# A hybrid attention block on one core: queries and merged outputs come back from device memory in 32x32 squares, turned on VectorE instead of TensorE

## The chip, the core and the metric

The kernel runs on one core of a Trainium2 chip. The metric is device time in microseconds of that core, as the median of several executions. The core has a matrix engine (TensorE, PE in the profile; its weight loads are PEld), three engines for elementwise work (VectorE is DVE, ScalarE is ACT, GpSimd is POOL), and a queue engine that only issues transfers (SyncE, SP). ACT and POOL issue transfers too, each in the order of its own instructions.

## What is computed

One block of a sequence model, in float32, for 256 tokens of width 2048 and 256 context tokens. The input is normalised and modulated by a vector c, and one large projection `w_in` gives everything else: attention queries, keys, values and gates, the inputs of a gated recurrence (HGRN, 16 heads, forward and backward), and two merge gates.

```python
aq, ak, av, ag, hq, hff, hfb, hi, hg, ma, mb = split_columns(xn @ w_in[l])
...
q = apply_axial_rope(aq.reshape(B, n, ATT_HEADS, ATT_HEAD_DIM), cos, sin) * q_scale
...
att_branch = window_attention(q, k, v, k_c, v_c, sink_logits[l]) * jax.nn.silu(ag)
...
y_a = hg_branch @ w_o_hgrn_l
y_b = att_branch @ w_o_attn_l
y = jax.nn.sigmoid(m_a + b_m[0]) * y_a + jax.nn.sigmoid(m_b + b_m[1]) * y_b
return y @ w_out_l
...
h = h + gate * merge_and_project(...)
return rmsnorm(h, final_norm_gain)
```

Two results of this text matter here. The rotated queries `q` (256 tokens, 16 heads of 128) are needed with the head's 128 columns on the partitions, but come out of the projection with tokens on the partitions. The merged `y` (256 x 2048) likewise comes out by tokens, and `y @ w_out` needs it by columns. Both have to be transposed.

## The kernel before

**Weights.** Every weight is streamed once, in chunks of 128 x 1024 floats. SP loads a chunk into one of five `raw` buffers (L66). ACT rounds it to the matrix engine's 32-bit format (`wh`, L85, three buffers), and DVE subtracts to get the remainder (`wl`, L86, three buffers). Activations are split the same way into `xH` and `xL`. PE multiplies three of the four combinations: high by high and low activation by high weight alternate (L100, L101), and the products with the low weight come last in a chunk (L103), so that `wl` may come later than `wh`. In the column-wise projections the like lines are L154 and L157. A token-wise projection of 512 columns (`proj_tok_g`) is eight such chunks; each step of the generator is one chunk.

**Stages.** First the modulation, the norms and the first projections; then eight steps, one for each pair of HGRN heads (some 740 to 1250 us in the profile); then the attention of 16 heads, woven with the projection `w_o_hgrn` (to about 1405 us); then `part_b`, four column blocks of the projection `w_o_attn` with the merge into `y` (to about 1490 us); then `w_out` and the output.

**Side work in the head pairs.** The recurrence of a pair leaves PE free in between, and a list of seventeen blocks (`side_work`) fills it: the four query blocks (`attn_queries(j)`, 512 columns, that is four heads), the attention gates, merge gates and output gates. After the projection of a query block DVE rotates each of the two token tiles (`rope`, L1092, L1097 and L1100) into a tile `qr` of 128 tokens x 512. `send` (L527) then issues the write of `qr` to a buffer `qr_dr` in device memory on ACT's queue, at the first chunk of the following block. When this has been issued the fetch becomes a task. Tasks are run three times a pair (`tasks_on`): the first call of a task fetches the tile (L1151, on POOL's queue), the next one turns it. `turn_tile` makes four PE transposes of 128 x 128 into PSUM (L1116, tile `tkt`); ACT scales and rounds it (L1118), DVE takes the remainder (L1119), and POOL writes both to `q_dr` (L1157), from which the attention loads them.

**The merge.** In `part_b(n)` DVE multiplies the projection of each token tile by its gate (L1424) and adds it to `y[n]` (L1425), 128 tokens x 512 columns. PE turns both tiles, four transposes each (L1431, tile `tky`), and ACT and DVE split them from PSUM (L1105, L1106) into the places of `xH` and `xL` that `w_out` reads. The buffers of merged `y` are later filled with four pieces `lw` of `w_out` (L1473, on POOL's queue), which DVE multiplies by the output gate (L1477).

**What sets the order.** PE's instructions stand in the order in which the program writes them through the head pairs and the attention (`manual_schedule`). The order of ACT, DVE, POOL and SP is set by a scheduler ahead of time, from its own estimate of the run and from priorities; `issue_after` and `behind_chunk` hold an instruction behind the splits of the newest weight chunk. On the chip each engine works through its list in order, and an instruction that waits holds up all that stand behind it on its engine.

Of the kernel before, what the change touches and what calls it, by code (L numbers as in the profile page):

```python
# [38 lines left out]
def block_kernel(ctx: ExitStack, tc: tile.TileContext, x, c, cx, c_ctx, w_ada, b_ada, norm_gain, w_in,  # L39
# [126 lines left out]
        return o[:, :T]  # L166


    cs = few.tile([P, K_END], F32, name="cs")
    ident = cs[:, K_ID: K_ID + P]  # L170
    mk = pad.tile([P, len(LEVELS), 32], U8, name="mk")
# [59 lines left out]
    ma_dr = [dram.tile([P, 1024], F32, name=f"ma{n}") for n in range(4)]  # L231
    mb_dr = [dram.tile([P, 1024], F32, name=f"mb{n}") for n in range(4)]
    kv_dr = [[dram.tile([P, 1024], F32, name=f"kv{i}_{t}") for t in range(2)] for i in range(2)]
    qr_dr = [dram.tile([P, 1024], F32, name=f"qr{j}") for j in range(4)]
    q_dr = [[dram.tile([P, 1024], F32, name=f"q{j}_{z}") for z in range(2)] for j in range(4)]
    ag_dr = [dram.tile([P, 1024], F32, name=f"ag{j}") for j in range(4)]

    FIRST = (("F0", 2), ("F1", 1), ("F0", 2))
# [874 lines left out]
    def turn_tile(src, dst, scale=1.0):  # L1113
        tk = ps.tile([P, 512], F32, tag="tp", name="tkt")
        for j in range(4):
            pe.transpose(tk[:, j * P: (j + 1) * P], src[:, j * HD: (j + 1) * HD], ident)  # L1116
        tk = tk.rearrange("p (r c) -> p r c", r=dst[0].shape[1])
        act.activation(dst[0], tk, AF.Copy, scale=scale)  # L1118
        dve.scalar_tensor_tensor(dst[1], tk, scale, dst[0].bitcast(F32), op0=ALU.mult, op1=ALU.subtract)  # L1119
# [27 lines left out]
    def attn_queries(j):  # L1147

        def fetch(t):
            qr = base.tile([P, 512], F32, tag="sm", name="qr", bufs=3)  # L1150
            nc.gpsimd.dma_start(qr, qr_dr[j][:, t * 512: (t + 1) * 512])  # L1151

            def then():
                q = [XL[:, 8 + 4 * z + 2 * t: 10 + 4 * z + 2 * t, :] for z in range(2)]
                turn_tile(qr, q, HD ** -0.5)
                for z in range(2):
                    nc.gpsimd.dma_start(q_dr[j][z][:, t * 512: (t + 1) * 512].rearrange("p (r c) -> p r c", r=2),  # L1157
                                        q[z].bitcast(F32))
            return then

        bq = yield from proj_tok_g(w_in, C_Q + 512 * j, x_st, range(2))
        for t in range(2):
            qr = base.tile([P, 512], F32, tag="sm", name="qr", bufs=3)
            rope(qr.rearrange("p (r h d) -> p r h d", r=2, h=2), bq[t], t)
            outs.append((qr_dr[j][:, t * 512: (t + 1) * 512], qr, lambda t=t: fetch(t)))

    def attn_gates(j):
        for hf in range(2):
# [248 lines left out]
            nc.sync.dma_start(fg[0], row_bcast(fin_gain[:1024], 1024))  # L1417
        nc.gpsimd.dma_start(gt[t], row_bcast(gate_rows[8 * t: 8 * t + 8, :], 1024))

    def part_b(n):  # L1420
        by = proj_tok(w_oa, n * 512, x_st, range(2))
        for t in range(2):
            yt = base.tile([P, 512], F32, tag="sm", name="yt", bufs=3)
            dve.tensor_tensor(yt, by[t], sgb[n][:, t, :], op=ALU.mult)  # L1424
            dve.tensor_tensor(y[n][:, t, :], y[n][:, t, :], yt, op=ALU.add)  # L1425

        tks = [ps.tile([P, 4, P], F32, tag=tg, name="tky") for tg in ("tp", "o")]
        with tc.manual_schedule(engines={mybir.EngineType.PE}):
            for t in range(2):
                for i in range(4):  # L1430
                    pe.transpose(tks[t][:, i, :], y[n][:, t, i * P: (i + 1) * P], ident)  # L1431
        for t in range(2):
            ks = slice(4 * n, 4 * n + 4)
            split(XH[:, ks, t * P: (t + 1) * P], XL[:, ks, t * P: (t + 1) * P], tks[t])

    def load_merge(n):
        sgb[n] = gt_tile(n, [P, 2, 512], "sgb")
        nc.gpsimd.dma_start(sgb[n].rearrange("p t c -> p (t c)"), mb_dr[n])

    load_merge(0)  # L1440
    for n in range(4):
        if n < 3:
            load_merge(n + 1)
        part_b(n)


    def y_st(kt, t):
# [131 lines left out]
```

## Time and profile before

| what | value |
|---|---|
| median of three runs | 1571.25 us (1571.19 to 1571.34) |
| profiled execution, its own time | 1573.59 us |
| its span, first to last instruction | 1571.8 us |
| granted TensorE clock, mean | 0.998 |
| transferred over the span | 339.99 MB in 232812 packets, mean 216 GB/s |
| query transposes on PE (L1116, cs and qr) | 32, the first at 859.8, the last at 1185.4 us |
| y transposes on PE (L1431) | 32, the first at 1409.7, the last at 1483.3 us |
| fetch of a query tile, issue to landing, median | 5.3 us (256 KB) |

A row of the profile names line, engine and operation, then the tile written and the tiles read, and how often. "x4" behind a row of the chain means that four instructions in a row are taken together. Behind `<-` in square brackets stands what ended the idle time before an instruction. A DMA's row on an engine is the time for issuing it; the transfer itself goes on behind.

### The profile page before, as it was taken

Reading aid. Unit: us, or ns where it says so; the run is one execution under the profiler, and the core shown is the slowest. Engines: PE = TensorE matmul, PEld = TensorE weight load, DVE = VectorE, ACT = ScalarE, POOL = GpSimd, SP = SyncE. Lnnn points to the kernel's source line nnn. Section 1 sums busy time; section 2 is a strip of 40 time slices with the busy share of each in tenths; the row PEclk is TensorE's granted clock in tenths of the full one; section 3 lists DMA queues with packets and bytes.
Section 4 is the critical chain, followed back from the end, with each engine's and each line's share of the span. In section 5 each row is a group of like instructions: output and inputs, shape, how many; then the busy total and the mean of one; then the engine's idle time right before and its main releaser. Section 6 shows DMA issues by size and latency. Waiting matters only on the chain.

```text
span 1571.8 us, 25977 instructions
## 1 busy us (share of the span) xinstructions
PE 1548.8 (99%) x9946; PEld 1291.8 (82%) x9946; DVE 1199.1 (76%) x1758; ACT 880.2 (56%) x1380; POOL 157.0 (10%) x298
## 2 busy tenths in 40 slices
PE   7999999999999999999999999999999999999998
PEld 4558888888888888888888888788888888888887
DVE  4448987777787878878888897887987777757664
ACT  4326545444555555665666666566566767744442
POOL 2000001110100000011212221121121000000000
PEclk9999999999999999999999999999999999999999
DMA  9996645656644444477786896877787744458661
GB/s 370 386 387 238 215 160 156 181 160 186 148 121 134 135 134 134 141 266 245 239 267 218 292 290 231 272 242 250 232 270 245 272 154 156 161 183 286 221 206 69
DMA packets 232812, 339.99 MB, mean 216 GB/s; under 512 B 12368, under 2 KB 137712, under 8 KB 231920
## 3 DMA queue, kind: packets, MB, share of 16 engines
q1 hardware_dynamic: 201808, 249.54, 48.6%
q0 software_dynamic: 21376, 70.38, 14.4%
q10 hardware_dynamic: 9504, 18.42, 3.3%
q8 instruction: 78, 1.28, 0.3%
q14 instruction: 46, 0.38, 0.1%
HBM read 300.53 MB, written 37.76 MB: 215 GB/s over the span
## 4 chain that ended last, share of the span: by engine, by line
PE 88%; DMA 4%; DVE 4%; issue 2%; ACT 1%; SPq 0%; POOL 0%; POOLq 0%; DVEq 0%; ACTq 0%
PE pj L100 13%; PE pj L101 12%; PE pj L103 12%; PE pj L154 7%; PE pj L759 5%; PE pm L759 4%; PE pj L157 4%; DMA raw<-in_w_in_dram 3%; PE pm L665 3%; PE pj L665 3%; PE pj L763 3%; PE pm L763 2%; PE pj L427 2%; PE pa L323 2%; DVE wl L641 2%
## 5 line engine op out<-in xcount | busy, mean ns | idle before, releaser
L85 ACT ACTIVATE wh<-raw 128x1024 fp32r<-128x1024 f32 x284 | 299.3, 1059 | 253.9 <-PE pj L101 157.0
L86 DVE TENSOR_TENSOR wl<-raw,wh 128x1024 fp32r<-128x1024 f32 x284 | 344.6, 1220 | 114.2 <-ACT wh L85 112.6
L100 PE MATMUL pj<-wh,xHL 128*128 128x512 f32 (+1 forms) x768 | 298.6, 390 | 0.0
L101 PE MATMUL pj<-wh,xHL 128*128 128x512 f32 (+1 forms) x768 | 294.8, 385 | 0.0
L103 PE MATMUL pj<-wl,xHL 128*128 128x512 f32 (+1 forms) x768 | 202.7, 386 | 0.0
L100 PEld LDWEIGHTS pj<-wh,xHL 128*128 128x128 f32 x768 | 144.4, 188 | 28.2 <-ACT sg L219 0.6
L101 PEld LDWEIGHTS pj<-wh,xHL 128*128 128x128 f32 x768 | 144.4, 188 | 27.6
L103 PEld LDWEIGHTS pj<-wl,xHL 128*128 128x128 f32 x768 | 142.0, 188 | 29.0
L640 ACT ACTIVATE wh<-raw 128x1024 fp32r<-128x1024 f32 x100 | 105.8, 1058 | 93.7 <-PE pj L759 37.3
L640 ACT ACTIVATE wh<-T 128x1024 fp32r<-128x1024 f32 x75 | 79.6, 1062 | 109.9 <-DVE T L621 24.1
L641 DVE TENSOR_TENSOR wl<-raw,wh 128x1024 fp32r<-128x1024 f32 x100 | 121.5, 1219 | 21.2 <-ACT wh L640 20.9
L154 PE MATMUL pj<-xHL,wh 128*128 128x512 f32 x512 | 130.2, 396 | 0.0
L154 PEld LDWEIGHTS pj<-xHL,wh 128*128 128x128 f32 x512 | 92.4, 189 | 16.8
L641 DVE TENSOR_TENSOR wl<-T,wh 128x1024 fp32r<-128x1024 f32 x75 | 91.4, 1219 | 13.8 <-ACT wh L640 13.7
L157 PEld LDWEIGHTS pj<-xHL,wl 128*128 128x128 f32 x512 | 69.8, 190 | 5.2
L157 PE MATMUL pj<-xHL,wl 128*128 128x256 f32 x512 | 71.3, 282 | 0.0
L932 DVE TENSOR_TENSOR A<-A,X 128x512 f32<-128x512 f32 x96 | 61.6, 682 | 0.2
L759 PE MATMUL pj<-wh,S 128*128 128x512 f32 x224 | 55.3, 389 | 0.0
L665 PE MATMUL pm<-S,wh 128*128 128x512 f32 x208 | 52.6, 395 | 1.6 <-ACT s L672 1.6
L665 PE MATMUL pj<-S,wh 128*128 128x512 f32 x208 | 52.5, 394 | 0.4 <-ACT s L672 0.4
L100 PE MATMUL pj<-wh,bH 128*128 128x512 f32 x128 | 50.2, 392 | 0.0
L101 PE MATMUL pj<-wh,bL 128*128 128x512 f32 x128 | 50.1, 391 | 0.0
(348 smaller groups left out, 2823.4 us busy)
## 6 DMA issues: line engine op xcount, KB each, us to landing
raw<-in_w_in_dram SPq DMA_DIRECT2D x300, 512.0 KB, 4.7
raw<-in_w_ada_dram SPq DMA_DIRECT2D x64, 512.0 KB, 8.0
raw<-in_w_o_hgrn_dram SPq DMA_DIRECT2D x32, 512.0 KB, 3.7
raw<-in_w_o_attn_dram SPq DMA_DIRECT2D x32, 512.0 KB, 4.3
raw<-in_w_out_dram SPq DMA_DIRECT2D x28, 512.0 KB, 4.4
hgw<-in_w_ada_dram POOLq DMA_DIRECT2D x32, 256.0 KB, 4.6
so<-in_w_ada_dram POOLq DMA_DIRECT2D x32, 256.0 KB, 4.9
F<-F POOLq DMA_DIRECT2D x16, 512.0 KB, 6.5
```

The costliest lines, as they stand in the source:

```text
L85: last_hi[0] = act.activation(h[:, :n], raw[:, :n], AF.Copy).ins
L86: last_lo[0] = dve.tensor_tensor(lo[:, :n], raw[:, :n], h[:, :n].bitcast(F32), op=ALU.subtract).ins
L100: pe.matmul(o, s[0], m[0], start=first, stop=False)
L101: pe.matmul(o, s[1], m[0], start=False, stop=False)
L103: pe.matmul(o, s[0], m[1], start=False, stop=last)
L154: pe.matmul(o.rearrange("p (a t) -> p a t", a=2), h[:, j, cs_], xHL[:, :, k0 + j, :T], start=k0 + j == 0, stop=False)
L157: pe.matmul(o[:, :T], lo[:, j, cs_], xH[:, k0 + j, :T], start=False, stop=k0 + j == KT - 1)
L640: act.activation(h, src, AF.Copy)
L641: dve.tensor_tensor(lo, src, h.bitcast(F32), op=ALU.subtract)
L665: pe.matmul(m_[z].rearrange("p (z a t) -> p z a t", z=2, a=2), h[:, k, :], mv(k), start=fresh and k == 0, stop=False, skip_group_check=True)
L759: pe.matmul(m_[z_][z], st_(4 * s + 2 * c + j)[:, a, z, :], h[:, j, :], start=fresh and c == 0 and j == 0 and a == 0, stop=False, skip_grou ...
L763: pe.matmul(m_[z_][z], st_(4 * s + 2 * c + j)[:, 0, z, :], lo[:, j, :], start=False, stop=c == 1 and j == 1, skip_group_check=True)
```

## The change

The query buffer `qr_dr[j]` now has 1024 rows of 128 floats, one for each token and head, and ACT writes a rotated tile as four such columns of rows. `load_squares` brings 512 of these rows back, already rearranged at the level of 32 x 32 squares: for each band of 32 columns one transfer takes the band from all 512 rows and puts its sixteen squares side by side on 32 partitions. That is four transfers a tile on ACT's queue, in pieces of 32 floats (128 bytes), 512 pieces each. What is left is to turn every square in place; DVE does that with one transpose instruction for the tile of 128 x 512, which works square by square. ACT and DVE then split the turned tile from SBUF, where before they read PSUM.

The first three blocks of `y` go the same way: POOL writes each merged tile to `y_dr[n]`, and during the next block's `part_b`, from its third chunk on, one step each loads the squares of the first tile, turns and splits them, loads those of the second, and turns and splits them. The last block is still turned on PE. The fetch on POOL (eight transfers) is gone, and so are 56 PE transposes.

```diff
--- before.py
+++ after.py
@@ -166,6 +166,13 @@
         return o[:, :T]
 
 
+    def load_squares(dst, src):
+
+
+        for a in range(4):
+            part = src[:, 32 * a: 32 * a + 32].rearrange("(n r) c -> r n c", r=32)
+            nc.scalar.dma_start(dst[32 * a: 32 * a + 32].rearrange("r (n c) -> r n c", c=32), part)
+
     cs = few.tile([P, K_END], F32, name="cs")
     ident = cs[:, K_ID: K_ID + P]
     mk = pad.tile([P, len(LEVELS), 32], U8, name="mk")
@@ -231,8 +238,9 @@
     ma_dr = [dram.tile([P, 1024], F32, name=f"ma{n}") for n in range(4)]
     mb_dr = [dram.tile([P, 1024], F32, name=f"mb{n}") for n in range(4)]
     kv_dr = [[dram.tile([P, 1024], F32, name=f"kv{i}_{t}") for t in range(2)] for i in range(2)]
-    qr_dr = [dram.tile([P, 1024], F32, name=f"qr{j}") for j in range(4)]
+    qr_dr = [dram.tile([1024, HD], F32, name=f"qr{j}") for j in range(4)]
     q_dr = [[dram.tile([P, 1024], F32, name=f"q{j}_{z}") for z in range(2)] for j in range(4)]
+    y_dr = [dram.tile([1024, HD], F32, name=f"y{n}") for n in range(3)]
     ag_dr = [dram.tile([P, 1024], F32, name=f"ag{j}") for j in range(4)]
 
     FIRST = (("F0", 2), ("F1", 1), ("F0", 2))
@@ -1148,11 +1156,17 @@
 
         def fetch(t):
             qr = base.tile([P, 512], F32, tag="sm", name="qr", bufs=3)
-            nc.gpsimd.dma_start(qr, qr_dr[j][:, t * 512: (t + 1) * 512])
+            with tc.issue_after(last_hi[0]):
+                load_squares(qr, qr_dr[j][t * 512: (t + 1) * 512, :])
 
             def then():
                 q = [XL[:, 8 + 4 * z + 2 * t: 10 + 4 * z + 2 * t, :] for z in range(2)]
-                turn_tile(qr, q, HD ** -0.5)
+                qt = base.tile([P, 512], F32, tag="sm", name="qt", bufs=3)
+                with behind_chunk():
+                    dve.transpose(qt, qr)
+                qv = qt.rearrange("p (r c) -> p r c", r=2)
+                act.activation(q[0], qv, AF.Copy, scale=HD ** -0.5)
+                dve.scalar_tensor_tensor(q[1], qv, HD ** -0.5, q[0].bitcast(F32), op0=ALU.mult, op1=ALU.subtract)
                 for z in range(2):
                     nc.gpsimd.dma_start(q_dr[j][z][:, t * 512: (t + 1) * 512].rearrange("p (r c) -> p r c", r=2),
                                         q[z].bitcast(F32))
@@ -1162,7 +1176,8 @@
         for t in range(2):
             qr = base.tile([P, 512], F32, tag="sm", name="qr", bufs=3)
             rope(qr.rearrange("p (r h d) -> p r h d", r=2, h=2), bq[t], t)
-            outs.append((qr_dr[j][:, t * 512: (t + 1) * 512], qr, lambda t=t: fetch(t)))
+            rows = qr_dr[j].rearrange("(t h p) c -> t p h c", t=2, h=4)[t]
+            outs.append((rows, qr.rearrange("p (h c) -> p h c", h=4), lambda t=t: fetch(t)))
 
     def attn_gates(j):
         for hf in range(2):
@@ -1417,12 +1432,32 @@
             nc.sync.dma_start(fg[0], row_bcast(fin_gain[:1024], 1024))
         nc.gpsimd.dma_start(gt[t], row_bcast(gate_rows[8 * t: 8 * t + 8, :], 1024))
 
-    def part_b(n):
-        by = proj_tok(w_oa, n * 512, x_st, range(2))
+    def squares(n):
+        for t in range(2):
+            sq = base.tile([P, 512], F32, tag="sm", name="ysq", bufs=3)
+            load_squares(sq, y_dr[n][t * 512: (t + 1) * 512, :])
+            yield
+            yT = base.tile([P, 512], F32, tag="bb", name="yT", bufs=2)
+            dve.transpose(yT, sq)
+            ks = slice(4 * n, 4 * n + 4)
+            split(XH[:, ks, t * P: (t + 1) * P], XL[:, ks, t * P: (t + 1) * P], yT.rearrange("p (k r) -> p k r", k=4))
+            yield
+
+    def part_b(n, turns):
+        parts = proj_tok_g(w_oa, n * 512, x_st, range(2))
+        for _ in range(8):
+            next(parts)
+            next(turns, None)
+        by = result(parts)
         for t in range(2):
             yt = base.tile([P, 512], F32, tag="sm", name="yt", bufs=3)
             dve.tensor_tensor(yt, by[t], sgb[n][:, t, :], op=ALU.mult)
             dve.tensor_tensor(y[n][:, t, :], y[n][:, t, :], yt, op=ALU.add)
+            if n < 3:
+                rows = y_dr[n].rearrange("(t k p) c -> t p k c", t=2, k=4)[t]
+                nc.gpsimd.dma_start(rows, y[n][:, t, :].rearrange("p (k c) -> p k c", k=4))
+        if n < 3:
+            return
 
         tks = [ps.tile([P, 4, P], F32, tag=tg, name="tky") for tg in ("tp", "o")]
         with tc.manual_schedule(engines={mybir.EngineType.PE}):
@@ -1433,6 +1468,11 @@
             ks = slice(4 * n, 4 * n + 4)
             split(XH[:, ks, t * P: (t + 1) * P], XL[:, ks, t * P: (t + 1) * P], tks[t])
 
+    def after_two(g):
+        yield
+        yield
+        yield from g
+
     def load_merge(n):
         sgb[n] = gt_tile(n, [P, 2, 512], "sgb")
         nc.gpsimd.dma_start(sgb[n].rearrange("p t c -> p (t c)"), mb_dr[n])
@@ -1441,7 +1481,7 @@
     for n in range(4):
         if n < 3:
             load_merge(n + 1)
-        part_b(n)
+        part_b(n, after_two(squares(n - 1)) if n else iter(()))
 
 
     def y_st(kt, t):
```

PE, behind the chunk during which the fifth query tile (first half of the third block) is turned. Before (`tkt` is the turned tile in PSUM, `cs` holds the identity, `pj` the projection's sums):

```order
L101 MATMUL pj<-wh,xHL 128x512
L103 MATMUL pj<-wl,xHL 128x512 x4
L1116 MATMUL tkt<-cs,qr 128x128 x4
L100 MATMUL pj<-wh,xHL 128x512
L101 MATMUL pj<-wh,xHL 128x512
```

In the list of the change the chunks follow each other without the transposes; nothing else of PE's list moves there.

ACT at the same query block, from the write of its two tiles on. Before:

```order
L85 ACTIVATE wh<-raw 128x1024
L527 DMA qr_133<-qr 128x512
L85 ACTIVATE wh<-raw 128x1024
L527 DMA qr_133<-qr 128x512
L859 ACTIVATE F_8296<-A 128x256 x4
L85 ACTIVATE wh<-raw 128x1024 x2
L862 ACTIVATE acc<-A 128x512
L862 ACTIVATE X_5762<-A 128x512
L85 ACTIVATE wh<-raw 128x1024
L1118 ACTIVATE xHL<-tkt 128x2x256
```

And in the change (`qr_133` is the buffer in device memory, `qt` the tile that DVE has turned):

```order
L85 ACTIVATE wh<-raw 128x1024
L535 DMA qr_133<-qr 128x4x128
L85 ACTIVATE wh<-raw 128x1024
L535 DMA qr_133<-qr 128x4x128
L174 DMA qr<-qr_133 32x16x32 x2
L867 ACTIVATE F_8302<-A 128x256 x4
L85 ACTIVATE wh<-raw 128x1024
L174 DMA qr<-qr_133 32x16x32 x2
L85 ACTIVATE wh<-raw 128x1024
L870 ACTIVATE acc<-A 128x512
L870 ACTIVATE X_5765<-A 128x512
L85 ACTIVATE wh<-raw 128x1024
```

The four loads of the first tile now stand among the weight splits, two and two, the first of them right behind the writes of the same rows.

DVE in `part_b`, where the first block of `y` is turned. Before:

```order
L1424 TENSOR_TENSOR yt<-pj,sgb 128x512
L86 TENSOR_TENSOR wl<-raw,wh 128x1024
L1425 TENSOR_TENSOR y<-y,yt 128x512
L86 TENSOR_TENSOR wl<-raw,wh 128x1024 x3
L1106 TENSOR_TENSOR xHL<-tky,xHL 128x4x128
L86 TENSOR_TENSOR wl<-raw,wh 128x1024
L1424 TENSOR_TENSOR yt<-pj,sgb 128x512 x2
L1477 TENSOR_TENSOR lw<-lw,gt 128x1024
L86 TENSOR_TENSOR wl<-raw,wh 128x1024
L1425 TENSOR_TENSOR y<-y,yt 128x512 x2
L86 TENSOR_TENSOR wl<-raw,wh 128x1024
```

And in the change (`ysq` holds the squares, `yT` the turned tile):

```order
L1454 TENSOR_TENSOR yt<-pj,sgb 128x512
L86 TENSOR_TENSOR wl<-raw,wh 128x1024
L1455 TENSOR_TENSOR y<-y,yt 128x512
L86 TENSOR_TENSOR wl<-raw,wh 128x1024 x3
L1441 STREAM_TRANSPOSE yT<-ysq 128x512
L86 TENSOR_TENSOR wl<-raw,wh 128x1024
L1114 TENSOR_TENSOR xHL<-yT,xHL 128x4x128
L1454 TENSOR_TENSOR yt<-pj,sgb 128x512 x2
L86 TENSOR_TENSOR wl<-raw,wh 128x1024
L1455 TENSOR_TENSOR y<-y,yt 128x512 x2
L86 TENSOR_TENSOR wl<-raw,wh 128x1024 x2
L1517 TENSOR_TENSOR lw<-lw,gt 128x1024
```

The transpose stands between two weight splits, and the split of the tile follows one chunk behind it; the sums and the `lw` product keep their places.

## The prediction

> **What bounds the kernel now.** I read the page first: busy time by engine, then the shares of the chain of waits.
>
> ```profile
> span 1571.8 us, 25977 instructions
> PE 1548.8 (99%) x9946; PEld 1291.8 (82%) x9946; DVE 1199.1 (76%) x1758; ACT 880.2 (56%) x1380; POOL 157.0 (10%) x298
> PE 88%; DMA 4%; DVE 4%; issue 2%; ACT 1%; SPq 0%; POOL 0%; POOLq 0%; DVEq 0%; ACTq 0%
> ```
>
> TensorE sets the time. Work taken off it shortens the kernel only while VectorE, the next busiest, keeps feeding it, so I asked for busy time in nine windows over the head pairs (the last row sums them) and in short ones around places where tiles are turned. Columns: window, us, busy time of PE, PEld, DVE, ACT, POOL, granted clock, share of the DMA engines, GB/s.
>
> ```profile
> sum 540.00, PE 537.93 PEld 461.35 DVE 448.04 ACT 344.93 POOL 102.68; mean PE 59.77 PEld 51.26 DVE 49.78 ACT 38.33 POOL 11.41
> ...
> 860.00:880.00 20.00, 20.00 (x216) 16.54 (x215) 20.00 (x30) 11.88 (x21) 7.32 (x16) 1.00 0.96 323
> 990.00:1010.00 20.00, 18.31 (x181) 14.70 (x180) 20.00 (x28) 10.82 (x16) 4.58 (x12) 1.00 0.80 262
> 1412.00:1424.00 12.00, 12.00 (x56) 9.95 (x55) 7.54 (x8) 5.64 (x6) 0.53 (x1) 1.00 0.99 388
> 1440.00:1485.00 45.00, 45.00 (x208) 37.43 (x207) 30.48 (x32) 19.73 (x22) 2.06 (x3) 1.00 0.65 218
> ```
>
> Over the 540 us PE is idle 2.07 us, DVE 92. But where query tiles are turned (860 to 880, 990 to 1010) DVE is busy for all 20 us, and the DMA engines for 0.80 to 0.96 of theirs. In part_b (from 1412) DVE has a third of its time free.
>
> **What is removed.** In the chain of waits, all fourteen removed groups stand on the path: eight of queries (tkt, L1116, four transposes each), then six of y, two of which stand singly and four in pairs (x8).
>
> ```profile
> 859.99 0.44 PE tkt L1116 x4
> 871.36 0.44 PE tkt L1116 x4
> ...
> 918.19 0.59 PE tkt L1116 x4
> 927.04 0.44 PE tkt L1116 x4
> ...
> 997.75 6.58 DMA qr<-qr
> ...
> 1004.47 0.63 PE tkt L1116 x4
> ...
> 1052.64 0.59 PE tkt L1116 x4
> ...
> 1138.18 0.63 PE tkt L1116 x4
> ...
> 1185.08 0.59 PE tkt L1116 x4
> ...
> 1409.90 0.44 PE tky L1431 x4
> ...
> 1423.32 0.44 PE tky L1431 x4
> ...
> 1438.53 0.87 PE tky L1431 x8
> ...
> 1460.05 0.87 PE tky L1431 x8
> ```
>
> The rows add to 4.35 us for queries and 2.62 us for y. The lengths of 0.59 and 0.63 hold some pipeline tail that a neighbour would show as well, so I count 0.44 for each group: 14 x 0.44 = 6.2 us, with 6.97 as the upper bound. At 1004.47 PE also stood still until the fetch of the query tile landed:
>
> ```profile
> 1004.47 0.63 PE L1116 MATMUL tkt<-cs,qr 128*128 128x128 f32 x4 [0.65 <-DMA qr<-qr]
> ```
>
> Nothing on PE depends on that landing after the change; the 0.65 us goes, if VectorE does not inherit it. Sum removed: 6.2 + 0.65 = 6.85 us.
>
> [...]
>
> **VectorE's turns.** Fourteen STREAM_TRANSPOSE of 128x512 f32 are added; the trace has none. Nearest rows: a 128x512 add from SBUF, and a weight subtraction of twice the size.
>
> ```profile
> L1100 DVE TENSOR_TENSOR qr<-qr,rt x8: 679/681/684, 751.4 to 1128.9; 128x512 f32<-128x512 f32 x8
> ...
> 1427.41 1.23 DVE L86 TENSOR_TENSOR wl<-raw,wh 128x1024 fp32r<-128x1024 f32 x1 [0.81 <-ACT wh L85]
> ```
>
> I take 0.68 us, since the shape is the same; bounds 0.34 (half) and 1.23 (as many bytes as the subtraction). What waits behind a turn in VectorE's order is the next wl, the low part of a weight chunk. In part_b the wl above ends at 1428.64 and PE asks for it at 1434.28; before the third query block another ends at 992.38 and is asked for at 994.59:
>
> ```profile
> 1434.28 1.07 PE L103 MATMUL pj<-wl,xHL 128*128 128x512 f32 x4
> ...
> 991.17 1.21 DVE L86 TENSOR_TENSOR wl<-raw,wh 128x1024 fp32r<-128x1024 f32 x1
> ...
> 994.59 1.07 PE L103 MATMUL pj<-wl,xHL 128*128 128x512 f32 x4
> ```
>
> The first and the last row make 5.6 us of lead in part_b and the other two 2.2 us at the thinnest. Both exceed 1.23, so the turns cost nothing by themselves; with the cover gone they would cost 14 x 0.68 = 9.5 us. The splits that follow only read SBUF instead of PSUM: nothing, either way.
>
> **The squares.** 56 DMA issues join ScalarE's queue, four per tile, and eight leave POOL's while six come (y's writes).
>
> ```profile
> L527 ACTq DMA_DIRECT2D qr<-qr x8: 326/326/327, 752.1 to 1129.6; - x8
> ...
> L1151 POOL DMA_DIRECT2D qr<-qr x8: 537/537/554, 827.6 to 1137.7; - x8
> ```
>
> 56 x 0.326 = 18.3 us more on ScalarE, which idles 44% of the span; in part_b it waits for PE to give a wh buffer back, 1.66 us a chunk, and four issues spread over three chunks (1.3 us) fit.
>
> ```profile
> 1429.04 1.06 ACT L85 ACTIVATE wh<-raw 128x1024 fp32r<-128x1024 f32 x1 [1.66 <-PE pj L101]
> ```
>
> A tile is 2048 packets of 128 bytes. Where weights arrive in 512-byte rows (430 to 630), 131 GB/s took a share of 0.45 of 16 engines:
>
> ```profile
> 430.00:630.00 200.00, 198.09 (x1126) 173.32 (x1125) 161.77 (x183) 114.78 (x148) 0.00 (x0) 1.00 0.45 131
> ...
> gate_rows<-grow POOLq DMA_DIRECT2D x1, 8.0 KB, 3.1
> qr<-qr ACTq DMA_DIRECT2D x8, 256.0 KB, 5.5
> ```
>
> 0.45 x 16 engines x 512 B / 131 GB/s = 28 ns a packet. A 128-byte packet costs from a quarter of this (7 ns) to as much: 0.9 to 3.6 us of 16 engines per tile. With 3.1 us, the landing of a DMA of hardly any data, a tile lands in 4.0 to 6.7 us; I take 6, nearer the end where a packet's price does not shrink, for the engines are shared.
>
> **Where they fall.** At the third query block the last of the first tile's four issues follows the wh below, so falls at 997.86 + 1.05 + 0.65 = 999.6; the split that uses the turned tile stood at 1005.14, the turn 0.7 us ahead of it.
>
> ```profile
> 993.01 0.33 ACTq L527 DMA_DIRECT2D qr<-qr  x1
> ...
> 996.62 1.34 ACT L859 ACTIVATE F<-A 128x256 f32<-128x256 f32 x4 [0.71 <-DVE A L932]
> 997.86 1.04 ACT L85 ACTIVATE wh<-raw 128x1024 fp32r<-128x1024 f32 x1
> ...
> 1005.14 0.60 ACT L1118 ACTIVATE xHL<-tkt 128x512 fp32r<-128x512 f32 x1
> ```
>
> Room 4.9 us against 6: late by 1.1, which the next wl's lead (2.2 or more) covers. The tightest tiles in part_b have about 5 us as well, by their places in the order, and 5.6 of lead.
>
> One new wait stands in ScalarE's own queue: the first squares must wait until the rotated queries have landed in device memory, issued near 993.0, landed 5.5 us later, 998.5. F (996.62) and the wh of 997.86 queue behind, up to 2.5 us late, at two tiles (third and fourth block). VectorE waits for F there and is full. Bounds 0 (leads cover it) to 2.5 each; leads of 2.2 leave 0.3, so I take 0.4 each: 0.8 us.
>
> Part_b has a wait of this kind on VectorE already: it stands 3.49 us for a row of w_out, between 1440 and 1485, where PE is busy for 45.00 of 45.00 us.
>
> ```profile
> 1444.41 1.23 DVE L1477 TENSOR_TENSOR lw<-lw,gt 128x1024 f32<-128x1024 f32 x1 [3.49 <-DMA lw<-in_w_out_dram]
> ...
> 1461.22 0.76 POOL L1473 DMA_DIRECT2D lw<-in_w_out_dram  x1 [23.42 <-PE tky L1431]
> ```
>
> So a tile of y that is 3 us late should be paid from lead too. Those lw loads reuse the buffers of merged tiles: as the POOL row shows, lw waited for PE's turns (tky) to be done with one. Now it waits until y's write has landed, and the write stands on POOL ahead of it. One wait takes the other's place, and I count nothing: 0 if they end together, and if lw comes 2 us later, VectorE's 3.49 becomes 5.5, while the lead left was 5.6 beside a wait of 3.49 already paid. Weight loads and squares also share the program's eight completion semaphores, so a late square can hold back the weight load that comes next on its semaphore; this is priced with the starved squares below.
>
> **Sum.** 6.85 - 0.8 = 6.05 us off the profiled execution's 1573.59; the median of the runs shown is 1571.25, 2.3 us below it, and the difference carries over: 1571.25 - 6.05 = **1565.2 us**. Own range 1563.6 (6.97 + 0.65 off, no stall) to 1568 (a further 2.8 us late at the two ScalarE holds).
>
> **Rivals.**
> *VectorE takes the queries' gain* (about 1570). DVE reads 20.00 of 20.00 around the query turns; eight turns of 0.68 = 5.4 us then replace 4.35 + 0.65 of PE, net +0.4, y still gives 2.6, and one hold costs its 2.5 us less the lead: 1571.25 + 0.4 - 2.6 + 0.3 = 1569.4, up to 1571 with both holds full. For it: those windows. Against: PE idles only 2.07 in 540, so the full windows are VectorE working ahead.
> *Starved squares* (about 1581). Small packets queue behind weight loads that fill 0.80 to 0.99 of the DMA engines. At three times my upper price a tile lands in 3.1 + 3 x 3.6 = 13.9 us; five tiles (first of the third and fourth query block, three in part_b) have room 4.9 + lead 5.6 = 10.5, so lose 3.4 each, 17 us in all: 1565.2 + 17 = 1582; less where leads are longer. It outweighs the gain from a landing of 11.7 us, and the kernel is measurably slower from 12.3. For it: the share 0.99 at 1412 to 1424. Against: 5.5 us for 256 KB at the same places.
> [...]
> *More than the sum* (1563.6): nothing stalls and the rows count whole. *No such change* is ruled out by the order: the turns are gone from PE's list.
>
> **How the numbers follow.** Forecast 0.60, VectorE's bound 0.17, starved squares 0.18, more than the sum 0.05. A measurement here tells 0.2% from nothing, 3.1 us: 1568.1 to 1574.4 counts as same. Faster 0.65, same 0.17, slower 0.18. The range reaches from 1562.8 (a little beyond the sum's bound) to 1576, which leaves out most of the starved case and little else.
>
> **What would show it.** PE's instructions fall by 56 and its idle time stays near 2 us over the head pairs; the turns read near 0.68 us; squares land in 4 to 7 us. Wrong: waits of PE for wl or wh that end with a DMA into qr or ysq, STREAM_TRANSPOSE idle before it for over 5 us, a landing above 12 us, or raw landing later than 4.7 us.

## The result: slower, by 0.67%

The changed kernel takes 1581.72 us (median of six runs, 1579.12 to 1587.36), the kernel before 1571.51 us (six runs, 1571.19 to 1573.85). The ratio is 1.0067, with a 95% interval of 1.0054 to 1.0079. The forecast was 1565.2 us with a range up to 1576. On another chip, later, the ratio was 1.0063 (1.0042 to 1.0084).

The profiled execution of the changed kernel took 1581.0 us. Its page: span, busy time, the DMA queues of POOL (q0) and ACT (q10) with packets and MB, and the shares of the chain of waits.

```profile
span 1579.2 us, 25958 instructions
PE 1547.8 (98%) x9890; PEld 1289.2 (82%) x9890; DVE 1206.0 (76%) x1772; ACT 879.1 (56%) x1380; POOL 157.2 (10%) x296
q0 software_dynamic: 21216, 69.85, 14.2%
q10 hardware_dynamic: 42144, 22.09, 4.9%
PE 83%; DMA 8%; DVE 5%; issue 2%; ACT 1%; SPq 0%; ACTq 0%; POOL 0%; DVEq 0%; POOLq 0%
```

The 56 matmuls are gone (9946 before, 9890 now), and the chain holds twice the share of DMA. What PE waited for between 740 and 1500 us (total, times, longest):

```profile
PE kt L998 <- DVE A L940: 6.0, 3, 4.0
PE pj L103 <- DVE wl L86: 4.5, 2, 2.3
```

Before, PE was idle in that stretch for about 2 us in all. Now it waits 10.5 us in these two rows, and each time for VectorE.

**Where the time went.** The sequence of weight chunks is the same in both kernels, so the start of a chunk's low products (L103) can be compared chunk by chunk. The table holds starts from the two traces, before and behind each place where the difference jumps. For one of them the rows can be seen: 1434.28 before (the row stands in the prediction), and after:

```profile
1442.88 1.20 PE L103 MATMUL pj<-wl,xHL 128*128 128x512 f32 x4 [2.23 <-DVE wl L86]
```

| low products start, before | after | difference | since the row above |
|---|---|---|---|
| 862.12 | 862.74 | +0.62 | |
| 929.15 | 928.25 | -0.90 | -1.52, turns removed |
| 940.03 | 941.58 | +1.55 | **+2.45, stall 1** |
| 1006.77 | 1007.13 | +0.37 | -1.18, turns and the wait of 0.65 removed |
| 1012.93 | 1015.90 | +2.98 | **+2.61, stall 2** |
| 1140.50 | 1142.35 | +1.85 | -1.13, turns removed |
| 1145.36 | 1152.87 | +7.51 | **+5.66, stall 3** |
| 1426.12 | 1432.33 | +6.21 | -1.30, turns removed |
| 1434.28 | 1442.88 | +8.60 | **+2.39, stall 4** |
| 1485.95 | 1493.36 | +7.41 | -1.19, turns removed |

Between the stalls 6.3 us came off. That is what the prediction's rows give for this stretch: thirteen of the fourteen groups at 0.44 us and the wait of 0.65 make 6.4. The four stalls cost 13.1 us. Stalls 2, 3 and 4 read like this on DVE (start, duration, instruction; in brackets the idle time before it and what ended it):

```profile
1010.26 0.71 DVE L1166 STREAM_TRANSPOSE qt<-qr 128x512 f32<-128x512 f32 x1 [3.25 <-DMA qr<-qr]
1010.89 1.25 DVE L940 TENSOR_TENSOR A<-A,X 128x512 f32<-128x512 f32 x2
...
1146.86 0.71 DVE L1166 STREAM_TRANSPOSE qt<-qr 128x512 f32<-128x512 f32 x1 [5.06 <-DMA qr<-qr]
...
1148.12 1.28 DVE L940 TENSOR_TENSOR A<-A,X 128x512 f32<-128x512 f32 x2
...
1441.01 0.71 DVE L1441 STREAM_TRANSPOSE yT<-ysq 128x512 f32<-128x512 f32 x1 [6.22 <-DMA ysq<-y]
1441.64 1.18 DVE L86 TENSOR_TENSOR wl<-raw,wh 128x1024 fp32r<-128x1024 f32 x1
```

DVE stands before a turn whose squares have not landed, for 3.25, 5.06 and 6.22 us. Behind the turn in its order stands what PE needs: the recurrence's `A` (L940) twice, the next `wl` (L86) once. In stalls 2 and 3 PE then pays a second time (PE's rows, and windows of 4 us behind them, whose granted clock is the third number from the right):

```profile
1011.60 0.44 PE L998 MATMUL kt<-cs,A 128*128 128x128 f32 x2 [1.91 <-DVE A L940]
...
1012.00:1016.00 4.00, 3.84 (x12) 3.08 (x12) 4.00 (x6) 1.35 (x4) 1.81 (x3) 0.57 0.85 236
1016.00:1020.00 4.00, 4.00 (x23) 3.48 (x22) 4.00 (x8) 3.10 (x9) 0.72 (x1) 1.00 1.02 351
...
1148.86 1.29 PE L998 MATMUL kt<-cs,A 128*128 128x128 f32 x4 [3.98 <-DVE A L940]
...
1149.00:1153.00 4.00, 4.00 (x13) 3.07 (x14) 4.00 (x6) 1.01 (x3) 1.31 (x3) 0.59 0.90 246
1153.00:1157.00 4.00, 4.00 (x23) 3.46 (x22) 4.00 (x8) 2.44 (x6) 1.26 (x2) 1.00 0.98 336
```

After an idle time of 3.98 us the granted clock is 0.59 over 4 us, and 13 matmuls start where 23 follow: 5.66 - 3.98 = 1.7 us more. Stall 2 has the same: 0.57 over 4 us, 12 matmuls where 23 follow. Its own waits come to 2.1 us, and before the change PE stood still for 1.16 us in the same chunk, for no cause that the profile shows. So waiting grew by 0.9 us only, and the other 1.7 of the 2.61 are the clock. The length of the wait alone does not tell when the clock falls: in stall 2 it fell after a wait of 1.91 us, and behind the waits of 2.29 and 2.23 us of stalls 1 and 4 it stayed at 1.00.

**Why the squares are late.** ScalarE's own queue shows it. Issue times of the squares (nanoseconds, least, median, longest), the longest issue, and the weight split that stood behind it:

```profile
L174 ACTq DMA_DIRECT2D qr<-qr x32: 309/470/2874, 840.2 to 1146.8; - x32
L174 ACTq DMA_DIRECT2D ysq<-y x24: 309/513/5705, 1422.1 to 1478.0; - x24
DMA to landing us min/median/max: 1.9/6.4/17.0
...
1424.38 5.71 ACTq L174 DMA_DIRECT2D ysq<-y  x1
1430.18 1.06 ACT L85 ACTIVATE wh<-raw 128x1024 fp32r<-128x1024 f32 x1 [4.75 <-PE pj L101]
```

One issue held ScalarE for 5.71 us, where 0.33 had been counted. The hold made that weight split late, but PE did not wait for it: between stalls 3 and 4 its rows show no wait. Nor does it make the tile late by much: the third of the four issues, at 1423.06, before the hold, landed at 1440.02, and the held one at 1440.99. And while the first tile of y was under way, the DMA queues moved this between 1426 and 1431 us (packets, MB, share of the time of 16 engines; q1 is SP's queue with the weights, q0 POOL's, q10 ScalarE's):

```profile
q1 hardware_dynamic: 484, 1.03, 53.2%
q0 software_dynamic: 242, 0.86, 43.3%
q10 hardware_dynamic: 483, 0.06, 7.9%
```

484 packets of the weights, 483 of the squares. The squares' packets are cheap: 0.079 x 16 x 5000 ns / 483 = 13 ns each, less than half of the 28 ns of a 512-byte packet (before, 430 to 630 us). But in these 5 us they advance one for each packet of the weights' queue, and those are large, 2.1 KB in the mean: 1.03 MB went by while the squares moved 0.06 MB. By an estimate from this pace, 97 packets a microsecond, a tile of 2048 packets needs 21 us. The pace did not hold to the end: from 1432 to 1436 us the squares' queue moved 1371 packets beside 607, and from 1436 to 1441, when hardly any of the tile was left, 86 beside 399. The counts are of all 16 engines together, so they do not show which engine had work of which queue, nor how an engine chooses between its queues; that POOL's queue, with 242, had work for all of that time is not shown either.

From the first issue of a tile's squares to the landing of the last, the trace gives 11.1 us for the first tile of the third query block, 11.8 for that of the fourth, and 18.9 for the first of y. DVE had come to the three turns 8.1, 6.8 and 12.7 us after the first issue. At the two query tiles the squares also stand in ScalarE's queue behind the write of the block's second tile, which landed at 1006.04 and 1140.58 us, when the squares had been issued from 998.93 and 1134.96 on.

### The profile page after: what moved, and what is told of

Same layout as the page of the kernel before. It is cut to its first block, busy times and chain, and to the rows that moved or that the text cites. A ratio compares the mean times of both kernels' runs of the same rounds, so it can differ in the third digit from the quotient of the medians.

```text
span 1579.2 us, 25958 instructions
## 1 busy us (share of the span) xinstructions
PE 1547.8 (98%) x9890; PEld 1289.2 (82%) x9890; DVE 1206.0 (76%) x1772; ACT 879.1 (56%) x1380; POOL 157.2 (10%) x296
## 3 DMA queue, kind: packets, MB, share of 16 engines
q0 software_dynamic: 21216, 69.85, 14.2%
## 4 chain that ended last, share of the span: by engine, by line
PE 83%; DMA 8%; DVE 5%; issue 2%; ACT 1%; SPq 0%; ACTq 0%; POOL 0%; DVEq 0%; POOLq 0%
PE pj L100 11%; PE pj L101 11%; PE pj L103 11%; PE pj L154 7%; PE pj L767 5%; PE pm L767 4%; PE pj L157 4%; DMA raw<-in_w_in_dram 4%; PE pj L771 3%; PE pm L673 2%; PE pm L771 2%; PE pj L673 2%; PE pj L435 2%; DVE wl L649 2%; PE pa L331 2%
## 5 line engine op out<-in xcount | busy, mean ns | idle before, releaser
L86 DVE TENSOR_TENSOR wl<-raw,wh 128x1024 fp32r<-128x1024 f32 x284 | 345.2, 1221 | 107.9 <-ACT wh L85 106.9
L103 PE MATMUL pj<-wl,xHL 128*128 128x512 f32 (+1 forms) x768 | 202.4, 386 | 4.5 <-DVE wl L86 4.5
L103 PEld LDWEIGHTS pj<-wl,xHL 128*128 128x128 f32 x768 | 141.9, 188 | 35.0 <-DVE wl L86 6.1
L154 PE MATMUL pj<-xHL,wh 128*128 128x512 f32 x512 | 130.3, 396 | 0.0
L154 PEld LDWEIGHTS pj<-xHL,wh 128*128 128x128 f32 x512 | 92.4, 189 | 17.0
L940 DVE TENSOR_TENSOR A<-A,X 128x512 f32<-128x512 f32 x96 | 61.8, 686 | 1.0 <-ACT Kmt L870 0.8
```

Of the source, the lines that this page charges most:

```text
L86: last_lo[0] = dve.tensor_tensor(lo[:, :n], raw[:, :n], h[:, :n].bitcast(F32), op=ALU.subtract).ins
L103: pe.matmul(o, s[0], m[1], start=False, stop=last)
L154: pe.matmul(o.rearrange("p (a t) -> p a t", a=2), h[:, j, cs_], xHL[:, :, k0 + j, :T], start=k0 + j == 0, stop=False)
```

## The experiments

The kernels below stand in the order in which they ran. The chips differ: on those of the experiments the kernel before takes 1574.4 to 1575.1 us, so ratios are given, each to the kernel before on the same chip.

### The queries alone, y alone

`q_only` turns y on PE as before, `y_only` the queries; the other half of the change stays.

> Only the queries return in squares; all four blocks of y are turned on PE again. Theory (squares land late and hold DVE, each at its own place): the three stalls of the head pairs stay (2.4 + 2.6 + 5.7 us) and eight groups of turns are saved (3.5 us): 1571.5 + 10.7 - 3.5 = 1578.5 us, range 1576 to 1582; no stall in part_b. Rival (the slowdown is made by the return of y and what it delays): 1568 us.

> Only y returns in squares; the queries are fetched by POOL and turned on PE as before. Theory (squares land late, each at its own place): one stall of 2.4 us in part_b against six groups saved (2.6 us): 1571.3 us, range 1569.5 to 1573. Rival (y makes the slowdown): 1578 us or more.

`q_only`: 1.0023 (1.0014 to 1.0033). `y_only`: 1.0018 (1.0007 to 1.0029). Neither half pays, and neither makes the slowdown alone. The stalls came each at its place. DVE's waits and PE's waits between 740 and 1500 us in `q_only`:

```profile
1010.60 0.71 DVE L1165 STREAM_TRANSPOSE qt<-qr 128x512 f32<-128x512 f32 x1 [3.10 <-DMA qr<-qr]
1145.33 0.71 DVE L1165 STREAM_TRANSPOSE qt<-qr 128x512 f32<-128x512 f32 x1 [4.79 <-DMA qr<-qr]
...
PE kt L997 <- DVE A L939: 5.3, 3, 3.6
PE pj L103 <- DVE wl L86: 0.9, 1, 0.9
```

and in `y_only`:

```profile
1434.29 0.71 DVE L1434 STREAM_TRANSPOSE yT<-ysq 128x512 f32<-128x512 f32 x1 [6.35 <-DMA raw<-in_w_o_attn_dram]
1474.68 0.71 DVE L1434 STREAM_TRANSPOSE yT<-ysq 128x512 f32<-128x512 f32 x1 [5.56 <-DMA ysq<-y]
...
PE pj L103 <- DVE wl L86: 2.5, 2, 1.4
```

For `q_only` 1.0045 had been expected (1578.5 to 1571.5) and 1.0023 came, its three stalls being shorter (PE waits 6.4 us in all, where the change waits 8.5 in the head pairs). For `y_only` no change had been expected and 1.0018 came, 2.8 us. A second tile (1474.68) was late as well: by the starts of the low products the two stalls cost 1.6 and 1.8 us, where 2.4 had been expected, so 1.0 us of the 2.8 is accounted for and the rest is not. (The first row names a weight load as what ended the wait. Squares and weight loads share completion semaphores: on each of eight the change's trace has 112 landings more than the trace before (56 transfers of 16 landings, over eight), and SP's weight loads wait there for squares seven times, 19.0 us in all, the longest 6.4.)

### Half as many packets

```diff
-            part = src[:, 32 * a: 32 * a + 32].rearrange("(n r) c -> r n c", r=32)
-            nc.scalar.dma_start(dst[32 * a: 32 * a + 32].rearrange("r (n c) -> r n c", c=32), part)
+            part = src[256 * (a // 2): 256 * (a // 2) + 256, 64 * (a % 2): 64 * (a % 2) + 64].rearrange("(n r) c -> r n c", r=32)
+            nc.scalar.dma_start(dst[32 * a: 32 * a + 32].rearrange("r (n c) -> r n c", c=64), part)
```

> The same bytes in four transfers a tile, with the order of every engine unchanged, but in 1024 pieces of 256 bytes where there were 2048 of 128; the tiles then hold other elements than the reference's. Theory (each small packet waits its turn behind a large one of another queue, so the landing goes with the number of packets): landing about halved (median near 4 us, longest near 10), ACT's longest issue below 3 us, the stalls at the third and fourth query block and at y's first tile shrink from 10.5 us to 3 us or less: about 1574 us, range 1571 to 1577. Rival (the turn stands in DVE's order where the tile cannot be there, whatever its packets; the time is latency, or wait for the write): landing as before and 1580 to 1583 us.

1.0004 (0.9995 to 1.0014): nearly all of the slowdown is gone, with the same bytes, the same number of transfers and the same orders. DVE's waits at the three places, and PE's:

```profile
1010.81 0.71 DVE L1166 STREAM_TRANSPOSE qt<-qr 128x512 f32<-128x512 f32 x1 [2.85 <-DMA qr<-qr]
1144.32 0.71 DVE L1166 STREAM_TRANSPOSE qt<-qr 128x512 f32<-128x512 f32 x1 [3.81 <-DMA qr<-qr]
1434.29 0.71 DVE L1441 STREAM_TRANSPOSE yT<-ysq 128x512 f32<-128x512 f32 x1 [1.50 <-DMA ysq<-y]
...
PE kt L998 <- DVE A L940: 3.8, 4, 2.4
PE pj L103 <- DVE wl L86: 1.5, 1, 1.5
DMA to landing us min/median/max: 3.2/6.0/12.0
```

PE waits 5.3 us instead of 10.5, and no issue takes longer than 1.56 us. But the landing was not halved, as had been expected: the median went from 6.4 to 6.0 us, the longest from 17.0 to 12.0. From first issue to last landing the three tiles took 10.4, 10.7 and 14.2 us instead of 11.1, 11.8 and 18.9. So the packets' number counts most in part_b; at the query tiles half as many packets took off about 1 us, which was enough to shrink the stalls. What the rest of a tile's time is, this run does not show; the write of the second query tile, ahead in the same queue, is one candidate.

### The turns later

```diff
-            return then
+            return lambda: then
```

and in `squares` the program asks for both tiles in the third and fourth chunk and for the turns from the sixth on, each turn behind a chunk's splits.

> The loads of the squares stay, but each turn stands later: a query tile is turned one task call (four weight chunks) later, a tile of y four or five chunks behind its load instead of one. Theory (DVE held by a turn whose tile has not landed is what PE feels): all stalls on squares go, at most the one that came from the shared ring of buffers stays (2.4 us): 1565 to 1570 us. Rival (ACT is what PE feels, being held up to 5.7 us by one issue): the turns do not wait any more but PE still stalls on wh or wl: 1576 us or more.

1.0005 (0.9995 to 1.0014), where 0.996 to 0.999 had been expected. The profiled execution, of 1580.91 us, is the slowest of the ten (their median is 1574.88), so its waits are no measure of the median. In the head pairs the edit did what it should: the first tiles of the third and fourth block, turned at 1065 (in the first row) and 1180, did not wait at all. In part_b the first tile was late as before (the last row sums up PE's waits for wl):

```profile
1065.36 0.70 DVE L1166 STREAM_TRANSPOSE qt<-qr 128x512 f32<-128x512 f32 x1
...
1434.09 0.71 DVE L1445 STREAM_TRANSPOSE yT<-ysq 128x512 f32<-128x512 f32 x1 [6.67 <-DMA ysq<-y]
...
PE pj L103 <- DVE wl L86: 5.9, 4, 3.0
```

But there the edit moved nothing: the scheduler put DVE's instructions of part_b into the same order as in the change, and DVE came to the first turn 11.8 us behind the first issue, where it had been 12.7. Whether more room would help in part_b is therefore not tested.

### No squares

`dve_only` keeps DVE's turns and takes the squares away: POOL fetches the query tiles as rows, as before the change, and y is turned straight from the merged tile. The writes of y to device memory go too, and the query tiles are written in whole rows again.

```diff
-            with tc.issue_after(last_hi[0]):
-                load_squares(qr, qr_dr[j][t * 512: (t + 1) * 512, :])
+            nc.gpsimd.dma_start(qr, qr_dr[j][:, t * 512: (t + 1) * 512])
...
-            dve.transpose(yT, sq)
+            dve.transpose(yT, y[n][:, t, :])
```

> The turns stay on DVE, the squares go: POOL fetches the query tiles as rows as before the change, and y's first three blocks are turned straight from the merged tile without a trip to device memory. Each 32 x 32 square is turned but the squares are not rearranged, so the values are others than the reference's. Theory (DVE's turns are free, all the loss is in how the squares arrive): the 6.2 us of PE come off and no stall is left but one from the shared ring of buffers: 4 to 7 us less than before (ratio 0.9955 to 0.9975). Rival (DVE, full around the query turns, pays for them itself): no less than 2 us below before, with PE waiting for wl or A around the turns.

0.9969 (0.9959 to 0.9980), as expected: with the turns on DVE and no squares 4.9 us come off. So DVE's turns are hidden, at 0.71 us each, also where DVE is full; the loss is in how the tiles get to device memory and back. One stall is left, and it is not the squares' (PE, then DVE before it):

```profile
942.17 1.20 PE L103 MATMUL pj<-wl,xHL 128*128 128x512 f32 x4 [1.49 <-DVE wl L86]
...
936.34 0.71 DVE L1164 STREAM_TRANSPOSE qt<-qr 128x512 f32<-128x512 f32 x1 [0.61 <-DMA ag<-sga]
938.52 1.27 DVE L812 TENSOR_TENSOR_SCAN e<-F,zero 128x255 f32<-128x255 f32 x2 [1.47 <-DMA ag<-sga]
```

The turn and the scan behind it wait for the write of a gate tile (`ag<-sga`). The turned tile `qt`, the scan's `e` and the gate tiles take turns in one ring of three buffers, and `qt` is new in it. Stall 1 of the change has the same two waits, of 0.88 and 1.91 us.

### Squares on the weights' own queue

```diff
-            nc.scalar.dma_start(dst[32 * a: 32 * a + 32].rearrange("r (n c) -> r n c", c=32), part)
+            nc.sync.dma_start(dst[32 * a: 32 * a + 32].rearrange("r (n c) -> r n c", c=32), part)
```

> The change, with the squares issued from SP, the queue that the weights use, instead of ACT. [...] Rival (a 128-byte piece is slow by itself): landing as before, the weights behind them late, ratio 1.006 or more.

0.9969 (0.9958 to 0.9979): faster than before, by as much as with no squares at all. The same packets, on SP's queue (issue and landing of the squares; then, between 1422 and 1425 us, the two queues that had work; then DVE's waits at the three places):

```profile
L174 SPq DMA_DIRECT2D ysq<-y x24: 328/488/4898, 1415.6 to 1465.9; - x24
DMA to landing us min/median/max: 2.0/6.2/10.4
...
q0 software_dynamic: 180, 0.61, 59.5%
q1 hardware_dynamic: 1353, 0.24, 43.8%
...
1008.89 0.71 DVE L1166 STREAM_TRANSPOSE qt<-qr 128x512 f32<-128x512 f32 x1 [1.01 <-DMA qr<-qr]
1140.73 0.71 DVE L1166 STREAM_TRANSPOSE qt<-qr 128x512 f32<-128x512 f32 x1 [1.68 <-DMA qr<-qr]
1426.86 0.71 DVE L1441 STREAM_TRANSPOSE yT<-ysq 128x512 f32<-128x512 f32 x1 [3.70 <-DMA ysq<-y]
```

In line with the weights the squares no longer go at one packet for each of theirs: the queue of both moved 1353 packets in 3 us, where ScalarE's moved 483 in 5. POOL's queue moved 180 in the same 3 us, of 3.4 KB in the mean, so the squares did not keep to one packet for each of that queue either. The longest landing falls from 17.0 to 10.4 us, a tile from first issue to last landing from 11.1 to 8.3 (third block), 11.8 to 8.1 (fourth) and 18.9 to 11.2 us (y's first). An issue can still hold its queue, for up to 4.9 us, but it is SP that is held, which has five buffers of weights ahead. The tiles had no more room than in the change: DVE came to the three turns 7.5, 6.6 and 7.6 us after the first issue. Around the two query turns DVE's order is that of the change; in part_b the first turn stands one chunk earlier. The median landing hardly moved (6.2 us); the late tiles did, and they made the stalls. If the pace beside another queue's packets (484 to 483) is what makes the squares late, a landing of 3 to 8 us, the longest under 10, and a ratio of 0.997 to 1.002 had been expected; the landing came a little longer, and the rival with the slow small piece is out.

### Queries alone, later; squares from POOL

> Queries alone in squares, y on PE as before, and each query tile turned one task call later. Theory (room is what the query tiles lack): of the three stalls of the head pairs (8.9 us of 10.7 with the slow clock behind them) those two that end with a landing go; eight groups save 3.5 us: ratio 0.9975 to 0.9995, with at most 2 us of PE idle time more than before between 740 and 1250 us. Rival (held ACT): PE stalls on wh or wl in the head pairs, ratio over 1.002.

`q_later` is `q_only` with the turn one task call later, as above: 0.9990 (0.9980 to 0.9999). The two stalls that end with a landing are gone, although an issue still held ScalarE for up to 2.1 us; PE waits 2.7 us in all, in four places, the longest (1.0 us, at 1218) with no issue of squares near it. In the head pairs, then, it was the turn that stood before its tile and not the held ScalarE.

> The change, with the squares issued from POOL. [...] Theory (turns by packet): a tile still lands in 6 us or more, longest over 10; DVE's turns wait as long as in the change, only ACT's wh are on time: 1576 to 1584 us. Rival (held ACT is what matters): about 1567 us.

`pool_queue` (one execution, 1574.66 us) met neither expectation. The order changed with it: the turns stand later in DVE's order, and do not wait at the places of stalls 2, 3 and 4, though squares land after 6.6 us in the median and up to 11.1.

```profile
1015.25 0.70 DVE L1166 STREAM_TRANSPOSE qt<-qr 128x512 f32<-128x512 f32 x1
1146.40 0.70 DVE L1166 STREAM_TRANSPOSE qt<-qr 128x512 f32<-128x512 f32 x1
1433.75 0.71 DVE L1441 STREAM_TRANSPOSE yT<-ysq 128x512 f32<-128x512 f32 x1
...
PE pj L103 <- DVE wl L86: 3.3, 1, 3.3
...
q0 software_dynamic: 23008, 73.52, 15.2%
q10 hardware_dynamic: 12576, 18.42, 3.3%
```

Only stall 1 is left, with 3.3 us. The last two rows, of POOL's and ScalarE's queue over the whole span, show what the theory had not counted with. Beside the change POOL's queue has gained 3.67 MB in 1792 packets, and ScalarE's has lost as many bytes in 29568: POOL's queue moved the same squares in packets of 2.0 KB in the mean. The three tiles took 9.1, 8.5 and 12.7 us from first issue to last landing. That fits the count of packets as the cause, but held ScalarE, late turns and small packets went away together, and this one execution does not tell them apart.

### The ring, and the best version

`sp_in_place` is `sp_queue` with the query tile turned in its own buffer; `sp_bb` has the turned tile in the ring of two buffers.

```diff
-                qt = base.tile([P, 512], F32, tag="sm", name="qt", bufs=3)
+                qt = qr
```

> Squares from SP, and DVE turns a query tile in its own buffer, so that the turn takes no second one of the three buffers that the gates and the scans share. Theory (the stall near 941 us comes from that ring: the turn and the scan behind it wait for gate tiles whose write has not landed): the PE stall near 941 us goes, 1.3 to 2 us more off than with the squares from SP alone: ratio 0.995 to 0.9965. Rival (that stall is the squares' or DVE's load): the stall stays and the ratio is 0.9965 to 0.998.

> Squares from SP, and the turned query tile in the other ring (two buffers, of the rotation and the sums) instead of the shared one of three. Theory of the ring: the stall near 941 us goes or shrinks below 0.6 us, ratio 0.995 to 0.9968; if this ring is the tighter one, a stall stands at another query tile. Rival: as with the squares from SP alone, 0.9965 to 0.998.

> The changed kernel once more, beside the two with the squares on SP and on the same chip. If the queue is the cause: ratio 1.004 to 1.008 again, with stalls of PE at the same four places (near 939, 1010, 1145 and 1441 us), and 0.9 to 1.2% slower than the two others. If its first timing was the chip's: ratio below 1.003.

`sp_in_place`: 0.9962 (0.9949 to 0.9975), 1568.42 us beside 1574.41. `sp_bb`: 0.9972 (0.9963 to 0.9982). `after_again`: 1.0063 (1.0042 to 1.0084), with PE's stalls at the same four places; by the medians it is 1.0% slower than `sp_in_place` and 0.8% than `sp_bb`. In `sp_in_place` nothing of note is left that PE waits for: between 740 and 1500 us its list of waits holds one, of 0.2 us. Stall 1 went with the second buffer, as the ring's theory says, though the scheduler moved the turn as well (it now starts at 919.98 us, in `sp_queue` at 938.65), so the buffer is not the only difference; in `sp_bb` it went too, and a smaller one of 0.8 us came at another tile. Between `sp_queue` and `sp_in_place` the intervals overlap, so the gain of the buffer is seen in the stall and not in the time. `sp_in_place` beats the kernel before by 0.25 to 0.51%.

## Why the prediction was wrong

**What is removed: right.** 6.2 us for fourteen groups and 0.65 for the wait at 1004, of which 6.4 fall between the stalls, where 6.3 us came off. In `sp_in_place`, where no stall is left, 6.0 us come off (0.38%), and the forecast was 6.05. That these two agree so closely is partly luck: the interval reaches from 3.9 to 8.0 us, and the 0.8 us which the forecast sets aside for ScalarE's holds was not measured there. The pipeline tail, for which the rows of 0.59 were counted as 0.44, shows in the change: the row of eight L154 matmuls that follows the recurrence's small ones (`al`) takes 2.04 us at 1055.62, the one at 1051.58, behind other projection rows, 1.84.

**VectorE's turns: right.** 0.71 us each, 0.68 had been taken, and `dve_only` shows them hidden. ScalarE's split of a turned tile takes 0.63 us from SBUF in the mean (L1168), where it took 0.60 from PSUM (L1118). The rival in which VectorE takes the queries' gain is out.

**The squares: this step failed, twice.** First, each issue was counted as 0.33 us, from ScalarE's other issues; it was 0.47 to 0.51 in the median and up to 5.71 us. The long issues stand behind others: the first issue of a tile took 0.31 to 0.35 us for 13 of 14 tiles, the three behind it up to 5.71. What it is that holds such an issue is not shown. Second, a landing of 6 us was taken for the tile, from the 3.1 us in which a DMA of 8 KB landed plus the packets' own time. The packets' time was right (13 ns, within the bounds of 7 to 28), and so was the median landing of one transfer (6.4), but the step let the tile have the 16 engines nearly for itself, and a tile needs the last of its four transfers. In part_b ScalarE's queue advanced one packet for each of the weights' queue for some 5 us, 483 beside 484, of 128 bytes and of 2.1 KB in the mean. From the first issue to the last landing a tile took 11.1, 11.8 and 18.9 us at the three places where DVE came to the turn after 8.1, 6.8 and 12.7. And the lead was measured on the wrong instruction at two of them: behind the query turns stood the recurrence's `A`, and not the next `wl`.

**The holds on ScalarE by the write's landing: right in kind, of no weight.** 0.8 us had been set aside; F (996.62 before) began at 1000.41, about 2 us later than the shift of that stage explains, and no stall began there. The write itself had grown slower, which had not been counted: it now goes in 512-byte pieces instead of 2 KB rows, and lands after 6.7 us in the median instead of 5.5. (The upper end of the prediction's own range adds 2.8 us for two holds; its bound of 2.5 us each would give 4.2 above the 0.8.)

**A wait not seen.** The turned tile takes a buffer of a ring that gate tiles leave only when their write has landed: 2.45 us at stall 1. The prediction named the turn's cost and not its buffer.

**The rivals.** The starved squares had 0.18, and they came: at the third and fourth block and in part_b, as named. Its price was wrong in its parts: it made the packet three times dearer and five tiles late by 3.4 us each, 17 us; there were three that PE felt, with 2.6 and 5.7 (1.7 of each the clock) and 2.4 us. That its 1581 us is so near the 1581.72 measured is therefore luck. The evidence against it, 5.5 us for 256 KB at the same places, was read wrongly: those 256 KB were 128 rows of 2 KB, a sixteenth of a tile's 2048 packets.

What stays open: at the two query tiles, how much of the late landing comes of the small packets beside the weights' queue and how much of the write of the second tile, ahead in the same queue. On SP's queue and on POOL's both went away together, and no run here has one without the other. The held ScalarE is not behind stall 4 by more than 1 us, since the transfer issued before the hold landed 0.97 us ahead of the held one.

## What to carry to other kernels

Count the packets of a transfer, and not its bytes alone, when it goes on a second queue beside a busy one. Here 2048 packets of 128 bytes on ScalarE's queue took 11.1 to 18.9 us beside the weights; half as many took 10.4 to 14.2, the same ones on the weights' own queue 8.1 to 11.2, and on POOL's queue, which moved them in packets of 2.0 KB in the mean, 8.5 to 12.7 (one execution). Keep such issues off an engine whose order cannot stand a held issue. Before an instruction that waits for a transfer is put into a full engine's order, compare the landing of the whole tile, from the first issue, with the time at which the engine comes to it and with the lead of what stands behind it, and count the buffer that its result takes. And look in the trace whether an instruction that was meant to stand later really does.

## What the runs showed of the hardware

- An issue of 512 small packets took 0.31 us at the least and up to 5.71 us, and held ScalarE for that time; SP it held for up to 4.9 us (`sp_queue`). POOL's 56 issues took 0.65 to 0.69 us (`pool_queue`).
- A 128-byte packet took 13 ns of a DMA engine (the change, 1426 to 1431 us), a 512-byte packet 28 (before, 430 to 630 us).
- The same 3.67 MB of squares made 29568 packets on ScalarE's or SP's queue and 1792 on POOL's.
- SP's and ScalarE's queues moved 484 and 483 packets in 5 us (the change, 1426 to 1431 us), of 2.1 KB in the mean and of 128 bytes; from 1432 to 1436 us it was 607 and 1371.
- After 3.98 us of idle time PE ran at a granted clock of 0.59 over 4 us, and after 1.91 us at 0.57 over 4 us, each of which added 1.7 us to the stall; after 2.29 and 2.23 us it stayed at 1.00.
